# Mixture of experts in a decoder layer: large experts as 128 split rows and 64 unsplit rows, another expert order, 16 KB weight pieces, 16-bit biases

## Chip, cores and metric

The kernel runs on one core of a Trainium2 chip. The metric is the time of one execution on the device in microseconds; a kernel's time is the median of its runs.

## What is computed

One decoder layer for 512 tokens of width 1024, in fp32: a token mixer (differential attention beside a gated MLP, one input and one output projection), a layer norm, a router that picks 4 of 32 experts for each token, the experts, a second layer norm. The change concerns the experts and the few steps ahead of them. Cut to that part, the reference is:

```python
logits = xt @ w_router + b_router
topv, topi = lax.top_k(logits, TOP_K)              # 4 of 32
gates = jax.nn.softmax(topv, axis=-1)
def expert_block(args):                            # rows of one expert
    xb, e = args
    h = xb @ w_up[e] + b_up[e]                     # 1024 -> 2 x 1024
    ...                                            # clamped SwiGLU -> 1024
    return a @ w_down[e] + b_down[e]               # 1024 -> 1024
```

Each token's output is the sum of its four experts' rows times their gates. An expert's weights are 8 MB for up (gate and linear columns) and 4 MB for down, so the layer reads some 400 MB of weights.

## The kernel before

**Exactness.** A matmul of fp32 operands is made in one of two ways. *Split*: the weights and the rows are each cut into a high part rounded to fp32r (a cast by ScalarE, L149) and a low rest (a subtraction by VectorE, L150), and three fp32r matmuls (high by high, high by low, low by high) are summed in PSUM. *Unsplit*: the fp32 weights go to TensorE as they are loaded, with 64 rows as stationary columns; the two halves of the output columns go to the two column halves of the array (`tiled_mm`, L1417), and no cast or subtraction is needed.

**Slots.** The experts are sorted by their number of rows on the device. One expert is fixed and comes first, the others follow in an order of ranks that is written into the kernel (`ORDER`); a rank has a fixed capacity (`CAP_STEPS`). Up to 64 rows make an *L* slot (16 of them), unsplit. 65 to 128 rows make an *M* slot (the fixed one and 11 more), split, six matmuls of 512 columns for each chunk (L1454 up, L1493 down). Over 128 rows make an *H* slot (ranks 1 to 4, capacities 256, 192, 176, 160): two row blocks, both split, on quarters of the up columns and halves of the down columns (`wide_mm`: L1344 for a full block; for a second block of up to 64 rows L1334 and L1338, whose stationary holds high and low rows side by side, so that the sum of the low half is later folded in by L1363 after a one-column matmul L1326).

**Chunks, loads and queues.** A slot has 16 up chunks and 8 down chunks of 128 by 1024 weights. The work list runs up of slot n, then down of slot n-1 (for H mixed in quarters). A slot's weights come as four up and two down loads of 2 MB into six raw buffers, released in order; SyncE issues the next load when the oldest buffer is released: at the split of its last chunk for M and H (`emit_splits`, `used`), after the last matmul for L. Splits are made three chunks ahead (LEAD). An M load takes two whole weight rows of a partition (16 KB) per piece (`wu_l`, `wd_l`), an L load 8 KB or 4 KB (`wu_t`, `wd_t`), an H load 1 KB or 2 KB (`wu_h`, `wd_h`, L675).

**PSUM.** PG holds the gate sums, PL the linear ones, PD the down sums, each 128 by 1024; X0 and X1 take transposes and lists. M and H use all of PG, PL and PD; an L slot uses one 512-column half, alternating. At the end of down, ScalarE scales PD into a buffer (`out_a`, L1400 for L and M, L1406 for H), and GpSimd scatters it into the accumulator in DRAM.

**Biases.** `bias_rows` makes a table from the up biases: a VectorE addition over 64 rows (L885), a cast to fp32r (L887), two subtractions (L890). An M slot adds them by two fp32r matmuls over 64 rows for gate and for linear (L1317), an L slot by two fp32 matmuls each (L1423), an H slot by L1322. `bias_rows` stands in the middle of the routing stretch: on ScalarE, L887 comes ahead of the copies L794 of the transposed hidden rows, which the router's matmul L799 needs; on VectorE, L885 and L890 come ahead of the second layer-norm tile (L777).

Of the kernel before, what the change touches and what calls it, by code (L numbers as in the profile page):

```python
# [34 lines left out]
CAP_STEPS = ((0, 128), (1, 256), (2, 192), (3, 176), (4, 160), (5, 128), (6, 120), (7, 112), (8, 104), (9, 96), (11, 88), (12, 80), (15, 72),  # L35
# [21 lines left out]
ORDER = "LLMLMHLMMMLMHLLMMLLLHMLLMLHLMLL"  # L57
# [9 lines left out]
def moe_layer(ctx, tc, x, w_in, lambda_q1, lambda_k1, lambda_q2, lambda_k2, subln_g, gmlp_ln_g,  # L67
# [10 lines left out]
    xb = [X0, X1]  # L78
    count = {}
# [5 lines left out]
    def xbank():  # L85
        return xb[nxt("x", 2)]
# [572 lines left out]
    wu_l = w_up[0].rearrange("e (p k) f -> e p k f", p=128)  # L659
    wu_h = w_up[0].rearrange("e (p k) (g c f) -> e p k g c f", p=128, g=2, c=4)  # L660
    wd_l = w_down[0].rearrange("e (p k) f -> e p k f", p=128)
    wd_h = w_down[0].rearrange("e (p k) (c f) -> e p k c f", p=128, c=2)
# [4 lines left out]
    def load_up(e, part, heavy, tiled=False):  # L667
        raw = raw_tile()
        if tiled:
            dst = raw.rearrange("p (k f) -> p k f", k=2)  # L670
            nc.sync.dma_start(dst, wu_t[e, :, part * 2:part * 2 + 2].rearrange("o p k f -> (o p) k f"))
        elif heavy:
            dst = raw.rearrange("p (k g f) -> p k g f", k=8, g=2)
            for g in range(2):
                nc.sync.dma_start(dst[:, :, g], wu_h[e, :, :, g, part].rearrange("o p k f -> (o p) k f"))  # L675
        else:
            dst = raw.rearrange("p (k f) -> p k f", k=2)
            nc.sync.dma_start(dst, wu_l[e, :, part * 2:part * 2 + 2].rearrange("o p k f -> (o p) k f"))
        return raw

    def load_down(e, part, heavy, pieces=1, tiled=False):
        raw = raw_tile()
        if tiled:
            src = wd_t[e, :, part * 4:part * 4 + 4]
            dst = raw.rearrange("p (k f) -> p k f", k=4)
        elif heavy:
            src = wd_h[e, :, :, part]
            dst = raw.rearrange("p (k f) -> p k f", k=8)
        else:
            src = wd_l[e, :, part * 4:part * 4 + 4]  # L690
            dst = raw.rearrange("p (k f) -> p k f", k=4)
        src = src.rearrange("o p k f -> (o p) k f")
        m = src.shape[1] // pieces
        for j in range(pieces):
            nc.sync.dma_start(dst[:, j * m:(j + 1) * m], src[:, j * m:(j + 1) * m])
        return raw
# [3 lines left out]
    x1v = x1.rearrange("p i (q k) -> p i q k", k=8)  # L700
    xrs = [view(W, i * 1024, 1024) for i in range(2)]
# [11 lines left out]
    tb = types.SimpleNamespace()  # L713
# [123 lines left out]
    def first_rows(i, ks):  # L837

        for k in ks:
            nc.tensor.matmul(xP[:, k], x1v[:, i, :, k], tb.oh0[:, i].bitcast(F32),  # L840
                             start=(i == 0 and k % 4 == 0), stop=(i == 3 and k % 4 == 3))
# [40 lines left out]
    def bias_rows():  # L882

        braw = tb.braw
# [10 lines left out]
    def first_loads(parts):  # L895
        for kind, part in parts:
            raw_of[(0, kind, part)] = (load_up if kind == "u" else load_down)(slot_expert(0), part, False)

    def norm_loads():
# [5 lines left out]
        tb.braw = view(tb.rt, 1024, 1024)  # L905
# [4 lines left out]
        for b in range(4):  # L910
            rows = slice(b * 32, (b + 1) * 32)
            nc.sync.dma_start(tb.braw[rows], b_up[0][:, (b // 2) * 1024:(b // 2) * 1024 + 1024])
# [67 lines left out]
    def first_x():  # L980

        xh, xl = t_buf(128, False)
        slots[0].xT.append((xh, xl))
# [64 lines left out]
    heavy = [r for r in range(1, NE) if capacity(r) > 128]  # L1048
    onehot = words("p64", 32, F32R)
    onehot_h = words("p64h", 2 * len(heavy), F32R).rearrange("p (g s) -> p g s", g=2)  # L1050
    onehot_t = words("p64t", 64).rearrange("p (g s) -> p g s", g=2)
# [70 lines left out]
    def tables_d():  # L1122
        P4 = tb.P4
        nc.vector.tensor_scalar(onehot_h[:, 1], P4[:, heavy[0]:heavy[-1] + 1], bge[:, 2:3], None, op0=OP.mult)
        nc.vector.tensor_tensor(onehot_h[:, 0], P4[:, heavy[0]:heavy[-1] + 1], onehot_h[:, 1].bitcast(F32),
                                op=OP.subtract)
        nc.vector.tensor_scalar(onehot_t[:, 1], P4, bge[:, 2:3], None, op0=OP.mult)
        nc.vector.tensor_tensor(onehot_t[:, 0], P4, onehot_t[:, 1], op=OP.subtract)
        tb.zeros = words("zeros", 128, BF16)
        nc.vector.memset(tb.zeros, 0.0)  # L1130
        tb.low_ident = words("lowid", 64, F32R)
        nc.vector.tensor_copy(tb.low_ident, ident[:, 64:128])

    def first_list():
# [4 lines left out]
        slots[0].lists.append((idx, gt))  # L1139
# [11 lines left out]
    def list_mask(s, blk, rows):  # L1151
        if blk == 0:
            nc.vector.tensor_tensor(tb.oh[:, :, 0:rows], iota[:, 0:rows].unsqueeze(1).to_broadcast([128, 4, rows]),
                                    tb.posm_s[:, :, s:s + 1].to_broadcast([128, 4, rows]), op=OP.is_equal)
            return
        for i in range(NT):
            nc.vector.tensor_scalar(tb.oh[:, i, 0:rows], iota[:, 0:rows], 128.0 * blk, tb.posm_s[:, i, s:s + 1],
                                    op0=OP.add, op1=OP.is_equal)
# [7 lines left out]
    def mask_h(s):  # L1166
        nc.vector.tensor_tensor(tb.oh.rearrange("p i (c r) -> p i c r", c=2),
                                iota[:, 0:64].unsqueeze(1).unsqueeze(1).to_broadcast([128, 4, 2, 64]),
                                tb.posm_s[:, :, s:s + 1].unsqueeze(3).to_broadcast([128, 4, 2, 64]), op=OP.is_equal)
# [27 lines left out]
    def transpose_h(src, eng, dst=None, js=slice(0, 4)):  # L1197
# [3 lines left out]
        tp = xbank().rearrange("p (j r) -> p j r", j=4)  # L1201
        for j in range(js.start, js.stop):
            nc.tensor.transpose(tp[:, j], src[:, j * 128:(j + 1) * 128], ident)
# [21 lines left out]
    def transpose_half(dst, src, hf, rows, stacked):  # L1225

        sv = src.rearrange("p (q k) -> p q k", k=8)
        tp = xbank()[:, 0:4 * rows].rearrange("p (k t) -> p k t", k=4)
        for k in range(4):
            nc.tensor.transpose(tp[:, k], sv[:, :, hf * 4 + k], ident[0:rows, 0:rows])  # L1230
        ks = slice(hf * 4, hf * 4 + 4)
        if stacked:
            split_to(dst[0][:, ks, 0:rows], dst[0][:, ks, 64:64 + rows], tp)
        else:
            split_to(dst[0][:, ks], dst[1][:, ks], tp)

    def t_buf(rows, stacked):
        j = nxt("tb", 4)
        hi = view(BC, j * 1024, 8, 128)
        if stacked:  # L1240
            return hi, view(words(f"low{j}", 1024), 0, 8, 64)
        return hi[:, :, 0:rows], view(words(f"low{j}", 1024, F32R), 0, 8, 128)[:, :, 0:rows]
# [6 lines left out]
    act2b = view(W, 2048, 2, 1024)  # L1249

    class Slot:
        def __init__(self, s):
            self.s = s
            self.nblk = (capacity(s) + 127) // 128
            self.rows = [min(128, capacity(s) - 128 * b) for b in range(self.nblk)]
            self.halves = [r <= 64 for r in self.rows]
            self.last = s == slot_order()[-1]

            self.tiled = self.halves[0]
            assert self.tiled or not self.last  # L1260
            h = slice(512, 1024) if self.tiled and nxt("tiled", 2) else slice(0, 512)
            self.hg, self.hl, self.hd = PG[:, h], PL[:, h], PD[:, h]
            self.down_psum = PD
            self.lists, self.xg, self.xT, self.aT, self.y = [], [], [], [], []

        def mask(self, b):
            if self.tiled:
                mask_h(self.s)
            else:
                list_mask(self.s, b, self.rows[b])  # L1270

        def fetch(self, b):
            if self.last:
                self.lists.append(full_list(self.s))
                self.xg.append(gather_h(self.lists[0][0]))
                return
            if self.tiled:
# [714 lines left out]
```

## Time and profile before

| | |
|---|---|
| runs | 1487.75, 1485.09, 1482.64 us, median 1485.09 us |
| profiled execution | 1484.02 us, span 1481.9 us, mean granted clock 0.978 |
| TensorE busy | 1404.2 us, 95% of the span |
| VectorE, ScalarE busy | 798.3 us (54%), 612.2 us (41%) |
| queue of the weight loads | 435.75 MB, 76.0% of 16 engines' span |
| experts on TensorE | first matmul at 274.1 us, last at about 1454.4 us |

An engine's busy time is what its instructions took; TensorE's matmuls overlap, so their price is the distance from one start to the next. The span begins with the first instruction; the execution's own time is 2.1 us longer than the span. The stretch before 274 us is the token mixer, the layer norm and the routing; after 1454 us comes the last accumulation and layer norm.

### The profile page before, as it was taken

How to read it: one execution, taken by the hardware profiler on the slowest of the kernel's cores; microseconds unless marked ns; L12 is line 12 of the kernel's file. 1: busy time of each engine (PE TensorE's matmuls, PEld its weight loads, DVE VectorE, ACT ScalarE, POOL GpSimd, SP SyncE). 2: the span in 40 equal slices, each digit the busy share in tenths (PEclk: the TensorE clock that was granted, in tenths of full speed). 3: DMA queues.
4: the chain of work that ended last, by engine and by line, in shares of the span. 5: the costliest groups of instructions: out<-in, count | busy, mean ns of one | idle time of the engine just before them, and what ended most of it. 6: DMA issues, size and time to landing. Idle time of an engine off the chain costs nothing. (4 is left out here: it accounts for less than half of the span.)

```text
span 1481.9 us, 17074 instructions
## 1 busy us (share of the span) xinstructions
PE 1404.2 (95%) x6494; PEld 872.9 (59%) x6494; DVE 798.3 (54%) x1237; ACT 612.2 (41%) x813; POOL 135.8 (9%) x136
## 2 busy tenths in 40 slices
PE   8999999899998999999999999996999999999992
PEld 6877778645655867675666545542666453656430
DVE  4455668643656545786855347531554363635324
ACT  3354541322544434574644345421454252526212
POOL 0000000032010010001100010010000120000210
PEclk9999999899999999999999999999999999999996
DMA  9030154569999979999996989999986999999994
GB/s 337 12 114 1 65 178 184 212 269 399 395 417 381 367 253 323 385 381 368 377 386 232 364 321 415 413 399 381 389 293 266 362 411 394 379 349 348 380 403 150
DMA packets 109717, 461.39 MB, mean 311 GB/s; under 512 B 7808, under 2 KB 41856, under 8 KB 84032
## 3 DMA queue, kind: packets, MB, share of 16 engines
q1 hardware_dynamic: 101328, 435.75, 76.0%
q0 software_dynamic: 8304, 24.52, 6.7%
q8 instruction: 52, 0.85, 0.2%
q14 instruction: 33, 0.27, 0.0%
HBM read 440.23 MB, written 20.00 MB: 311 GB/s over the span
## 5 line engine op out<-in xcount | busy, mean ns | idle before, releaser
L150 DVE TENSOR_TENSOR ring<-raw,ring 128x1024 fp32r<-128x1024 f32 (+1 forms) x400 | 468.6, 1208 | 178.3 <-ACT ring L149 172.2
L149 ACT CAST ring<-raw 128x1024 fp32r<-128x1024 f32 (+1 forms) x400 | 400.9, 1039 | 144.3 <-DMA raw<-in_w_up_dram 24.0
L1417 PE MATMUL PG<-raw,low 128*64 128x512 f32 x512 | 135.1, 605 | 5.3 <-DMA raw<-in_w_up_dram 3.1
L1417 PE MATMUL PL<-raw,low 128*64 128x512 f32 x512 | 132.9, 597 | 0.0
L1417 PE MATMUL PD<-raw,low 128*64 128x512 f32 x512 | 124.2, 616 | 3.2 <-DMA raw<-in_w_down_dram 1.7
L1382 ACT ACTIVATE PG<-PG 128x512 f32<-128x512 f32 (+9 forms) x37 | 26.1, 706 | 203.6 <-PE PG L1417 122.5
L150 DVE TENSOR_TENSOR low<-X,bc 128x512 fp32r<-128x512 f32 (+7 forms) x66 | 39.5, 599 | 130.9 <-ACT bc L149 130.9
L1454 PE MATMUL PG<-ring,bc 128*80 128x512 f32 (+7 forms) x384 | 108.5, 404 | 1.4 <-DVE ring L150 0.9
L1493 PE MATMUL PD<-ring,bc 128*80 128x512 f32 (+7 forms) x384 | 107.2, 400 | 2.3 <-ACT ring L149 1.7
L1454 PE MATMUL PL<-ring,bc 128*80 128x512 f32 (+7 forms) x384 | 107.0, 401 | 1.7 <-DVE w L1387 1.7
L149 ACT CAST bc<-X 128x512 fp32r<-128x512 f32 (+10 forms) x78 | 37.8, 484 | 145.0 <-PE X L1230 144.4
L1454 PEld LDWEIGHTS PG<-ring,bc 128*80 128x80 f32 (+7 forms) x384 | 60.5, 165 | 32.1 <-issue 7.9
L1454 PEld LDWEIGHTS PL<-ring,bc 128*80 128x80 f32 (+7 forms) x384 | 61.2, 165 | 29.8 <-issue 4.9
L1493 PEld LDWEIGHTS PD<-ring,bc 128*80 128x80 f32 (+7 forms) x384 | 60.8, 164 | 30.6 <-ACT PG L1382 3.2
L1383 DVE TENSOR_SCALAR w<-PL 128x512 f32<-128x512 f32 (+9 forms) x36 | 30.1, 836 | 86.8 <-PE PL L1454 39.9
L1230 PEld LDWEIGHTS X<-ident,w 128*128 128x128 f32 (+10 forms) x304 | 41.5, 197 | 55.2 <-issue 26.2
L1417 PEld LDWEIGHTS PL<-raw,low 128*64 128x64 f32 x512 | 35.2, 137 | 63.0 <-issue 62.3
L1417 PEld LDWEIGHTS PD<-raw,low 128*64 128x64 f32 x512 | 33.9, 140 | 60.6 <-issue 55.4
L1417 PEld LDWEIGHTS PG<-raw,low 128*64 128x64 f32 x512 | 32.8, 136 | 61.3 <-issue 53.1
L1189 POOL DMA_INDIRECT w<-x1d,small x15 | 18.1, 1207 | 553.5 <-DMA raw<-in_w_up_dram 276.0
L1230 PE MATMUL X<-ident,w 128*128 128x128 f32 (+10 forms) x304 | 49.9, 287 | 12.4 <-DVE low L150 12.4
L1454 PE MATMUL PG<-ring,low 128*80 128x512 f32 (+7 forms) x192 | 60.4, 396 | 0.3 <-DVE low L985 0.3
(497 smaller groups left out, 2167.1 us busy)
## 6 DMA issues: line engine op xcount, KB each, us to landing
raw<-in_w_up_dram SPq DMA_DIRECT2D x112, 2048.0 KB, 13.4
raw<-in_w_down_dram SPq DMA_DIRECT2D x64, 2048.0 KB, 14.1
raw<-in_w_up_dram SPq DMA_DIRECT2D x32, 1024.0 KB, 15.9
raw<-in_w_in_dram SPq DMA_DIRECT2D x8, 1024.0 KB, 11.5
raw<-in_w_o_dram SPq DMA_DIRECT2D x2, 2048.0 KB, 9.0
raw<-in_x_dram SPq DMA_DIRECT2D x4, 512.0 KB, 6.4
raw<-in_w_in_dram SPq DMA_DIRECT2D x4, 512.0 KB, 9.2
w<-in_x_dram SPq DMA_DIRECT2D x4, 512.0 KB
```

Of the source, the lines that this page charges most:

```text
L149: nc.scalar.copy(hi, src)
L150: eng.tensor_tensor(lo, src, hi.bitcast(F32), op=OP.subtract)
L1189: nc.gpsimd.indirect_dma_start(out=xg, out_offset=None, in_=x1d_h, in_offset=bass.IndirectOffsetOnAxis(ap=idx, axis=0))
L1230: nc.tensor.transpose(tp[:, k], sv[:, :, hf * 4 + k], ident[0:rows, 0:rows])
L1382: nc.scalar.activation(pg, pg, AF.Silu, scale=SWIGLU)
L1383: nc.vector.tensor_scalar(l, pl, LIMIT + 1.0, 1.0 - LIMIT, op0=OP.min, op1=OP.max)
L1417: nc.tensor.matmul(P[64 * c:64 * c + 64], T[:, k], w[:, c * 512:(c + 1) * 512], start=(k == 0 and not started), stop=(k == 7))
L1454: nc.tensor.matmul(P[:, cs], x_[:, kt], w_[:, cs], start=(kt == 0 and n == 0), stop=(kt == 7 and n == 2))
L1493: nc.tensor.matmul(P[:, cs], a_[:, k], w_[:, cs], start=(k == 0 and n == 0), stop=(k == 7 and n == 2))
```

## The change

H slots get one capacity, 192. The first 128 rows are split as in an M slot (`full_mm`), the other 64 rows are unsplit as in an L slot (`half_mm`), and both are made for each chunk of weights: six fp32r matmuls and one pair of fp32 column-half matmuls. The 64 rows' gate and linear sums lie in the halves of PD and their down sum in X1; an L slot ahead of an H slot also puts its down sum in X1, and transposes have X0 alone meanwhile. An H load's buffer is released after its last matmul rather than at its split. The order is new, with no two H side by side and no H after an M. Every load now takes 16 KB of contiguous weights per partition (`wu_v`, `wd_v`), so the transposes of rows pick strided columns. The bias table becomes three bf16 rows (high, middle, low) of 2048 columns for each expert, added for all slots by bf16 matmuls over 96 rows (`half_bias`, `full_bias`).

```diff
-CAP_STEPS = ((0, 128), (1, 256), (2, 192), (3, 176), (4, 160), (5, 128), ...
+CAP_STEPS = ((0, 128), (1, 192), (5, 128), ...
-ORDER = "LLMLMHLMMMLMHLLMMLLLHMLLMLHLMLL"
+ORDER = "LMLHLMLMLMLHLMLMLMLHLMLMMLMLHLL"
+assert "HH" not in ORDER and "MH" not in ORDER and ORDER[-1] == "L"
...
-    wu_t = w_up[0].rearrange("e (k p) f -> e p k f", p=128)
-    wd_t = w_down[0].rearrange("e (k p) f -> e p k f", p=128)
+    wu_v = w_up[0].rearrange("e (c p j) f -> e c p j f", c=2, j=4)
+    wd_v = w_down[0].rearrange("e (c p j) f -> e c p j f", c=2, j=4)
...
     def bias_rows():
-        nc.vector.tensor_scalar_add(braw[64:128], braw[64:128], 1.0)
-        tb.bup = bup = words("bup", 1024, F32R)
-        nc.scalar.copy(bup, braw)
-        for b in (1, 3):
-            rows = slice(b * 32, (b + 1) * 32)
-            nc.vector.tensor_tensor(bup[rows], braw[rows], bup[rows].bitcast(F32), op=OP.subtract)
+        tb.bup = bup = words("bup", 2048, BF16)
+        nc.vector.tensor_scalar_add(tb.braw[1], tb.braw[1], 1.0)
+        for n in range(2):
+            b, part = tb.braw[n], bup[0:96, n * 1024:n * 1024 + 1024]
+            nc.scalar.copy(part, b)
+            for p0 in (32, 64):
+                rows = slice(p0, p0 + 32)
+                nc.vector.tensor_tensor(b[rows], b[rows], part[rows], op=OP.subtract)
+                nc.scalar.copy(part[rows], b[rows])
+            rows = slice(64, 96)
+            nc.vector.tensor_tensor(b[rows], b[rows], part[rows], op=OP.subtract)
+            nc.scalar.copy(part[rows], b[rows])
...
+            if self.wide:
+                self.hg, self.hl, self.hd = PD[:, 0:512], PD[:, 512:1024], X1
+            elif self.half:
+                h = slice(512, 1024) if nxt("tiled", 2) else slice(0, 512)
+                self.hg, self.hl, self.hd = PG[:, h], PL[:, h], PD[:, h]
+                if not self.last and capacity(order[n + 1]) > 128:
+                    self.hd = X1
...
+                    def mm(w, hi, lo, kt=kt, gl=gl):
+                        if self.full:
+                            P = (PG, PL)[gl]
+                            if kt == 7:
+                                self.full_bias(P, gl)
+                            self.full_mm(P, self.xT[0], kt, hi, lo)
+                        if self.half:
                             P = (self.hg, self.hl)[gl]
-                            self.tiled_mm(P, self.xT[0], kt, w)
+                            self.half_mm(P, self.xT[-1], kt, w)
                             if kt == 0:
-                                self.tiled_bias(P, gl)
+                                self.half_bias(P, gl)
...
-                ready[emitted[0]] = split_ring(src(raw_of[key + (part,)]), *shape)
-                used(key + (part,))
+                ready[emitted[0]] = (raw,) + split_ring(raw, *shape)
+                if not slots[key[0]].half:
+                    used(key + (part,))
```

**Where instructions move.** The first place is `bias_rows` on ScalarE, in the routing stretch. Before, one cast of the bias table stands ahead of the copies of the hidden rows:

```order
134 L153 CAST bc_71<-X_65 128x4x128
135 L887 CAST bup_1644<-ring_48_1528 128x1024
136 L794 COPY ring_46_1526<-X_64 128x512
137 L794 COPY ring_46_1526<-X_65 128x512
138 L800 COPY r_109<-X_64 128x32
```

With the change, eight stand there (L774 is the copy that was L794):

```order
135 L869 CAST bup_1643<-ring_46_1526 96x1024
136 L873 CAST bup_1643<-ring_46_1526 32x1024 x2
137 L876 CAST bup_1643<-ring_46_1526 32x1024
138 L869 CAST bup_1643<-ring_44_1524 96x1024
139 L873 CAST bup_1643<-ring_44_1524 32x1024 x2
140 L876 CAST bup_1643<-ring_44_1524 32x1024
141 L774 COPY ring_44_1524<-X_64 128x512
142 L774 COPY ring_44_1524<-X_65 128x512
```

On VectorE in the same place, the change has one addition (L866) and six subtractions ahead of the next layer-norm tile (L757, which was L777), where before it were one addition and two subtractions:

```order
282 L866 TENSOR_SCALAR ring_44_1524<-ring_44_1524 96x1024
283 L872 TENSOR_TENSOR ring_46_1526<-ring_46_1526,bup_1643 32x1024 x2
284 L875 TENSOR_TENSOR ring_46_1526<-ring_46_1526,bup_1643 32x1024
285 L872 TENSOR_TENSOR ring_44_1524<-ring_44_1524,bup_1643 32x1024 x2
286 L875 TENSOR_TENSOR ring_44_1524<-ring_44_1524,bup_1643 32x1024
287 L757 SCALAR_TENSOR_TENSOR w_76<-w_76,PG 128x1024
```

So each of these queues carries a chain in which cast and subtraction take turns, ahead of work that the router waits for. The other place is an H slot on TensorE. Before, two row blocks share a chunk (the last rows of an up quarter and the fold of the one before it):

```order
1720 L1363 MATMUL PG<-ring_60_1980,lowid_2071 64x512
1721 L1344 MATMUL PL<-ring_53_1831,bc_71 128x512 x2
1722 L1344 MATMUL PL<-ring_53_1831,low_169_4775 128x512
1723 L1334 MATMUL PL<-ring_53_1831,bc_71 128x512
1724 L1338 MATMUL PL<-ring_53_1831,bc_71 64x512
```

With the change, the end of the down chunks of the slot before (PD) and the first up chunks of the H slot:

```order
1111 L1347 MATMUL PD<-ring_60_2053,bc_71 128x512 x4
1112 L1347 MATMUL PD<-ring_60_2053,low_87_2656 128x512 x2
1113 L1347 MATMUL PG<-ring_54_1969,bc_71 128x512 x4
1114 L1347 MATMUL PG<-ring_54_1969,low_92_2736 128x512 x2
1115 L1333 MATMUL PD<-raw_86_2654,low_94_2783 64x512 x2
1116 L1340 LDWEIGHTS p_36_674
1117 L1340 MATMUL PD<-bup_1643,p_36_674 64x512
1118 L1340 LDWEIGHTS p_36_674
1119 L1340 MATMUL PD<-bup_1643,p_36_674 64x512
1120 L1347 MATMUL PL<-ring_58_1991,bc_71 128x512 x4
1121 L1347 MATMUL PL<-ring_58_1991,low_92_2736 128x512 x2
1122 L1333 MATMUL PD<-raw_86_2654,low_94_2783 64x512 x2
```

Fp32r matmuls (L1347) and fp32 column-half matmuls (L1333) now alternate in every chunk of an H slot, and the first L1333 writes the PD that the down chunks just ahead have filled.

## Rows read from the trace of the kernel before

**Rows 1.** Busy time in the expert stretch: stretch, length, busy time (instructions) by engine, clock, DMA.
```profile
274.10:1454.40 1180.30, 1147.23 (x5180) 662.16 (x5180) 621.29 (x801) 502.81 (x596) 130.22 (x116) 0.99 0.96 360
```

**Rows 2.** Waits of TensorE between 280 and 1450 us: total us, times, longest us.
```profile
PE X L1230 <- DVE low L150: 12.4, 3, 7.9
...
PE PG L1417 <- DMA raw<-in_w_up_dram: 3.1, 3, 1.5
...
PE PD L1417 <- DMA raw<-in_w_down_dram: 1.7, 2, 1.0
...
PE PD L1417 <- ACT k L1400: 1.2, 1, 1.2
```

**Rows 3.** Routing stretch on VectorE: start, duration, engine, line, operation, count.
```profile
222.88 0.69 DVE L885 TENSOR_SCALAR ring<-ring 64x1024 f32<-64x1024 f32 x1
224.69 2.47 DVE L890 TENSOR_TENSOR bup<-ring,bup 32x1024 fp32r<-32x1024 f32 x2 [1.12 <-ACT bup L887]
227.18 1.22 DVE L777 SCALAR_TENSOR_TENSOR w<-w,PG 128x1024 f32<-128x1024 f32 x1
```

**Rows 4.** The same stretch on ScalarE.
```profile
223.60 1.05 ACT L887 CAST bup<-ring 128x1024 fp32r<-128x1024 f32 x1 [4.36 <-DVE ring L885]
224.56 1.06 ACT L794 COPY ring<-X 128x512 f32<-128x512 f32 x2
```

**Rows 5.** The same stretch on TensorE.
```profile
226.35 1.87 PE L799 MATMUL X<-r,ring 128*128 128x32 f32 x16
...
249.16 0.43 PE L824 MATMUL X<-k,oh 128*128 128x96 f32 x2 [1.52 <-DVE k L817]
```

**Rows 6.** TensorE after a long wait, timeline of 472 to 478 us.
```profile
476.51 1.12 PE L1230 MATMUL X<-ident,w 128*128 128x128 f32 x4 [3.74 <-DVE low L150]
```

**Rows 7.** Busy time after that wait (columns as in the first group).
```profile
478.00:482.00 4.00, 4.00 (x12) 0.95 (x8) 1.92 (x3) 0.25 (x1) 0.00 (x0) 0.56 1.02 429
```

**Rows 8.** TensorE in an L slot, timeline from 1426 us.
```profile
1427.71 1.03 PE L1423 MATMUL PG<-bup,p64t 128*64 128x512 f32 x4
1428.57 1.03 PE L1417 MATMUL PL<-raw,low 128*64 128x512 f32 x4
```

**Rows 9.** TensorE in an M slot's last up chunks, timeline from 303 us.
```profile
303.58 0.73 PE L1317 MATMUL PG<-bup,p 64*128 64x512 f32 x2
...
305.83 0.73 PE L1317 MATMUL PL<-bup,p 64*128 64x512 f32 x2
```

**Rows 10.** TensorE in an H slot, timeline from 1308 us.
```profile
1308.93 0.44 PE L1363 MATMUL PG<-ring,lowid 32*64 32x512 f32 x1
1309.30 0.73 PE L1344 MATMUL PL<-ring,bc 128*128 128x512 f32 x2
1309.87 0.40 PE L1344 MATMUL PL<-ring,low 128*128 128x512 f32 x1
1310.10 0.39 PE L1334 MATMUL PL<-ring,bc 128*128 128x512 f32 x1
```

**Rows 11.** TensorE where L work meets M work, timeline from 1405 us.
```profile
1405.61 1.03 PE L1417 MATMUL PL<-raw,low 128*64 128x512 f32 x4
1406.57 1.15 PE L1493 MATMUL PD<-ring,bc 128*72 128x512 f32 x4
...
1408.02 1.08 PE L1493 MATMUL PD<-ring,bc 128*72 128x512 f32 x4
```

**Rows 12.** TensorE where M work meets L work, timeline from 465 us.
```profile
465.33 0.62 PE L1454 MATMUL PL<-ring,low 128*120 128x512 f32 x2
465.88 1.94 PE L1417 MATMUL PD<-raw,low 128*64 128x512 f32 x8
```

**Rows 13.** Weight queue from 963 to 1029 us, L slots: packets, MB, share of 16 engines.
```profile
q1 hardware_dynamic: 4900, 24.20, 91.6%
```

**Rows 14.** Weight queue from 596 to 640 us, M slots.
```profile
q1 hardware_dynamic: 1104, 16.17, 89.7%
```

**Rows 15.** Weight queue from 1043 to 1063 us, an H slot.
```profile
q1 hardware_dynamic: 4744, 7.06, 99.8%
```

More of the change, by code (lines that the diff above doesn't have):

```diff
@@ L1045, in routing @@
         nc.sync.dma_start(bd, b_down[0])
[L1048 to L1051, printed above, removed]
+    onehot = words("p64", 32, BF16)
     def counts():
@@ L1248, in moe_layer, with __init__ @@
     act2 = [view(W, 2048, 1024), view(W, 3072, 1024)]
-    act2b = view(W, 2048, 2, 1024)
     class Slot:
-        def __init__(self, s):
+        def __init__(self, n, s):
+            order = slot_order()
             self.s = s
[L1254 to L1264, printed above, removed]
+            cap = capacity(s)
+            self.full = 0 if cap <= 64 else min(128, cap)
+            self.half = cap <= 64 or cap > 128
+            self.wide = cap > 128
+            assert cap <= 192
+            self.last = n == len(order) - 1
+            assert not (self.last and self.full)
+            self.parts = [0, 128] if self.wide else [0]
+            if self.wide:
[5 more added lines that the diff above has]
+                    self.hd = X1
+            self.nparts = len(self.parts)
+            self.lists, self.xg, self.xT, self.aT, self.y = ([None] * self.nparts for _ in range(5))
@@ L1266, in mask, with is_half @@
+        def is_half(self, b):
+            return self.half and b == self.nparts - 1
         def mask(self, b):
-            if self.tiled:
-                mask_h(self.s)
+            if self.is_half(b):
+                mask_h(self.s, self.parts[b])
             else:
-                list_mask(self.s, b, self.rows[b])
+                list_mask(self.s, self.full)
         def fetch(self, b):
             if self.last:
-                self.lists.append(full_list(self.s))
-                self.xg.append(gather_h(self.lists[0][0]))
-                return
@@ new lines, in full_mm, with full_bias @@
+        def full_mm(self, P, T, k, hi, lo):
+            xh, xl = T
+            for n, (x_, w_) in enumerate(((xh, hi), (xh, lo), (xl, hi))):
+                for c in range(2):
+                    cs = slice(c * 512, (c + 1) * 512)
+                    nc.tensor.matmul(P[0:self.full, cs], x_[:, k], w_[:, cs], start=(k == 0 and n == 0),
+                                     stop=(k == 7 and n == 2))
+        def full_bias(self, P, gl):
+            lhs = onehot[0:96, self.s:self.s + 1].to_broadcast([96, self.full])
+            for c in range(2):
+                c0 = gl * 1024 + c * 512
+                nc.tensor.matmul(P[0:self.full, c * 512:c * 512 + 512], lhs, tb.bup[0:96, c0:c0 + 512], start=False,
+                                 stop=False)
@@ new lines, in down_chunks, with mm, src @@
+            for k in range(KT):
+                def mm(w, hi, lo, k=k):
+                    if self.hd_taken():
+                        tb.x1_taken = True
+                    if self.full:
+                        self.full_mm(PD, self.aT[0], k, hi, lo)
+                    if self.half:
+                        self.half_mm(self.hd, self.aT[-1], k, w, self.last)
+                def src(t, k=k):
+                    return t[:, (k % 4) * 1024:(k % 4) * 1024 + 1024]
+                out_.append((k // 4, src, (1024,) if self.full else None, mm))
@@ L1512, in down_chunks @@
             return out_
-    slots = [Slot(r) for r in slot_order()]
+    slots = [Slot(n, s) for n, s in enumerate(slot_order())]
     N = len(slots)
@@ L1636, in at @@
         events.setdefault(c, []).append((lead, f))
-    def place_folds(every=False):
-        while folds and (every or len(stream) >= folds[0][0] + folds[0][3]):
-            after, key, (copies, mm), _ = folds.pop(0)
-            where[key] = len(stream)
-            stream.append((None, (after, copies, None, mm)))
     def add(n, kind, part):
@@ L1653, in add @@
             stream.append(((n, kind), c))
[L1654 to L1662 removed]
+        if part == ch[-1][0]:
+            where[(n, kind, "sum")] = len(stream) - 1
     chunks = {}
@@ L1707, in moe_layer @@
+        c = where[(n, "d", "sum")]
+        at(c, lambda sl=sl: sl.out_a(), LEAD)
+        at(c + 1, lambda sl=sl: sl.out_b(), L)
     ready = {}
@@ L1711, in moe_layer @@
     for key, (part, *_) in stream:
[L1712 to L1713 removed]
+        uses[key + (part,)] = uses.get(key + (part,), 0) + 1
     def used(load):
@@ L1877, in moe_layer @@
             mm(*ready.pop(c))
-            if key is not None and shape is None:
+            if slots[key[0]].half:
                 used(key + (part,))
```

429 lines of the change are left out of this document (119 added, 310 removed).

## The prediction

> **What bounds the kernel now.** The busy times of the engines come first: TensorE is busy for most of the span. The same view of the expert stretch alone says where it isn't: 1147.2 of 1180.3 us, with the DMA engines at 0.96 too [rows 1]. So TensorE sets the pace, and the weight loads are so close behind that each microsecond taken from TensorE must be checked against them. The table of TensorE's waits then says what stops it: it names VectorE's low part for 12.4 us and loads directly for 3.1 and 1.7 us [rows 2]. Followed back, the 12.4 us are late weights as well, since the transposes stand behind splits that wait for a buffer: 17.2 us in all. Behind such a wait TensorE is slow: after 3.74 us of idleness [rows 6] the granted clock of the next 4 us is 0.56 of the upper level of 2.4 GHz, so mostly the lower one, 1.2 [rows 7]; 4 x 0.44 makes some 2 us. There were two such waits, 4 us. Last, the timelines give prices as distances between starts.
>
> **Unit prices.** An fp32r matmul of 512 columns takes 0.23 us [rows 10]. A pair of unsplit matmuls for an L chunk takes 0.86 us, and so does an L bias [rows 8]. Two M biases with the six matmuls between them take 2.25 us [rows 9]; less 6 x 0.23 = 1.38 this leaves 0.87 for a bias and what it does to its neighbours. Where L work meets M work the last L chunk takes 0.96 instead of 0.86 and the first M chunk 1.45 instead of 1.38 [rows 11]. The other way, the last two M matmuls take 0.55 instead of 0.46, and the next two L chunks last 1.94 us instead of 1.03 + 0.86 [rows 12, 8]. The round trip costs 0.10 + 0.07 + 0.09 + 0.05 = 0.31 us, one way 0.155.
>
> **The change, term by term.**
>
> *1. The bias table: +12 us.* Only the routing stretch pays it. VectorE's addition ends at 223.57 [rows 3]. After it the two queues take turns: a subtraction lasts 2.47 / 2 = 1.23 us [rows 3], a cast 1.05 [rows 4]. Subtract, subtract (226.1), cast (227.2), subtract (228.4), cast (229.5), the second half's first cast (230.6), subtract, subtract (233.1), cast (234.2), subtract (235.4), cast (236.5). Then the copies of hidden rows, 1.06 us [rows 4], end at 237.6. The router's matmul, which began at 226.35 [rows 5], is in order on TensorE, so all projections behind it wait 11.3 us; VectorE's next tile moves from 227.18 [rows 3] to 235.4 only. Some 2 us at the lower clock follow [rows 7]. TensorE had 1.52 us to spare where it next met VectorE [rows 5], which covers that much: 11.3 + 2 - 1.5 = 12. Ends: 0, if the matmuls make it up before the tail of the routing, which VectorE sets; +16, if the narrower casts cost more.
>
> *2. L biases in bf16: -19 us.* There are 16 x 2 of them. An fp32 bias costs 0.86 [rows 8]. No row shows a bf16 matmul of this width; the nearest is fp32r's 0.23 [rows 10], and the two column halves may run side by side as the fp32 pair does. I take 0.25: 32 x 0.61 = 19. Ends: -21 (0.20) and 0, should it take the fp32 time.
>
> *3. M biases over 96 rows: -10 us.* 12 x 2 of them, from 0.87 [rows 9] to two matmuls of 0.23 without the step to a 64-row stationary: 24 x 0.41 = 10. Ends 0 (the step is paid for 96 rows too) and -13.
>
> *4. H arithmetic: -28 us.* Before: three experts of 48 steps x 5 matmuls and one of 48 x 6, 1008 x 0.23 = 232; 64 half-width biases at half of that, 7; 18 folds at 0.37 [rows 10], 7; 18 one-column matmuls, taken at 0.1, 2. Sum 248. After: 4 x 24 chunks x (1.38 + 0.86) = 215, and 4 x 2 x (0.46 + 0.25) = 6 for biases. Sum 221, so about -28. A further 32 transposes of 128 columns go, a quarter of 0.23 each: -2.
>
> *5. Type changes: +26 us.* Counted along the program, work passes between unsplit and split chunks 49 times before and 215 times after, of which 188 are inside H slots: 166 x 0.155 = 26. Ends: +14 if weights of the next chunk are loaded under the last one, +55 if each costs twice as much, as the fp32 stationaries here belong to other row sets. The Trainium skill's page TensorEngine Tiling (Array Packing), section Key Properties, says that a change of tiling mode drains TensorE, which speaks against exactly this mixing; by it nothing of the 26 could be hidden. The trace agrees in that each passage costs something [rows 11, 12].
>
> *6. PD's eviction: +2 us.* The first L1333 of an H slot writes the PD which the M slot before it just filled. In the same situation TensorE once waited 1.2 us for ScalarE's eviction [rows 2]. Here 1.38 us of L1347 lie between, which cover most; half a microsecond for each of four slots. Ends 0 and +8 (two casts of 1.05 ahead of the eviction). Behind that wait stands all of the H slot.
>
> *7. Weights in time: -4 us.* The queue moved 24.20 MB in 66 us at 91.6% [rows 13], 16.17 MB in 44 at 89.7% [rows 14], 7.06 MB in 20 at 99.8% [rows 15]: 400, 410 and 354 GB/s at full share. With 16 KB pieces all should do 410 and leave a tenth to gathers and scatters: 12.58 MB in 34 us. An L slot then has 25 us on TensorE, an M slot 36, an H slot 62. Three pairs of L and M and one L between two H slots lack 3 x 7 + 9 = 30 us, and an H slot refills 28, with what the six buffers hold beyond it. That is just about even: I leave 4 us of waiting in each of four stretches, 16, against 17.2 + 4 before. Ends -21 and +10. The Trainium skill's page DMA: Bandwidth & Descriptors, section Specifications, puts line rate at 512 bytes and up; by that alone larger pieces bring nothing, this term would be 0 and the sum -19. Here the 1 KB pieces ran at 354 GB/s and the 16 KB ones at 410, so the trace differs.
>
> Sum: 12 - 19 - 10 - 28 - 2 + 26 + 2 - 4 = -23, against the profiled execution's 1484.0 us (span 1481.9 and 2.1 us around it): 1461. That execution lies 1.1 us under the median of the runs, so the forecast is **1462 us**.
>
> **Rivals.**
> - *Prefetch runs out: 1478 us.* An H part now holds its buffer until its last matmul, some three chunks of 2.5 us later than at its split. If the 7.5 us of lead that this costs is missing at the end of two of the four stretches, 16 us come on top: 1478. For it speaks the DMA's 0.96; against it that H slots bring 28 us of slack each.
> - *H slots pay for mixing: 1492 us, slower.* In each of 96 H chunks the step to unsplit columns and back costs 0.63 us instead of 0.31: +30. It decides from +0.29 us a chunk, where the gain of 23 and the bound of measurement are used up. For it: the rows price only changes between long runs of one type. Against it: rows 11 and 12 have the same stationaries and moving types.
> - *The routing delay is hidden and waits vanish: 1442 us.* The 12 us shrink to 5 and the waiting to 3: -20. For it: the spare time at the next meeting with VectorE; against it: the whole chain is serial.
> - *The change does not do what it says*: bf16 biases that run at the fp32 price give back 19 us, 1481.
>
> **How the numbers follow.** Forecast (1452 to 1472): 0.55. Prefetch runs out: 0.15. Mixing: 0.13. Routing hidden: 0.12. Biases at the old price: 0.05. The range 1441 to 1488 takes in all but the slow case and the outer parts of the others. About 0.3%, or 4.4 us, is what a measurement here tells from no change: faster means under 1480.7. The forecast and the hidden case count as faster, with two thirds of the prefetch case and half of the last: 0.79. Within the bound: the rest of these and a little of the mixing case, 0.10. Slower: 0.11.
>
> **What would show it.** Right: the router's matmul at about 237.6, behind casts, and a lower clock after it; an L bias at a quarter of an L chunk; an H chunk of 2.5 us, evenly; TensorE's waits in the expert stretch at 15 to 20 us, at the end of stretches of L and M. Wrong: an H chunk over 2.85 us, waits for loads over 35 us, a routing stretch that is no later, or an L bias still at 0.86 us.

## The result, and the profile after

The changed kernel takes 1448.51 us (median of 4 runs, 1446.65 to 1449.89) against 1485.17 before in the same session: ratio 0.9753, 95% interval [0.9735, 0.9772]. The forecast was 1462 in a range of 1441 to 1488. The direction was right and the time lies in the range, but 37 us went where 23 were forecast.

The profiled execution has a span of 1448.2 us, 33.7 less than before. Three marks divide the difference: the first expert matmul, the last up chunk of the last expert, and the end. The stretch between the first two (columns as in rows 1), before:

```profile
274.10:1441.95 1167.85, 1137.45 (x5136) 659.16 (x5138) 617.43 (x790) 496.14 (x583) 130.22 (x116) 0.99 0.96 360
```

and after:

```profile
290.55:1400.76 1110.21, 1098.02 (x4925) 588.95 (x4927) 608.69 (x756) 479.11 (x537) 111.38 (x108) 1.00 0.95 379
```

The experts lost 57.6 us (1167.85 less 1110.21), of which 39.4 are TensorE's busy time and 18.2 its idleness. Ahead of them 16.4 us were added, behind them 7.5 (39.95 us from the second mark to the end before, 47.44 after): -57.6 + 16.4 + 7.5 = -33.7.

TensorE's waits from 280 to 1450 us, the answer to [rows 2]:

```profile
PE PD L1678 <- DMA w<-accd,r: 13.6, 1, 13.6
PE X L1687 <- DVE small L1685: 6.7, 1, 6.7
PE PD L1347 <- ACT ring L152: 3.3, 2, 1.7
PE X L1075 <- DVE r L835: 3.2, 1, 3.2
...
PE PG L1333 <- DMA raw<-in_w_up_dram: 1.1, 2, 0.6
PE X L1179 <- DVE low L1180: 0.8, 1, 0.8
```

Under the names that made 17.2 us before, late weights are 1.9 us now (1.1 and 0.8). The two waits on a cast, 3.3 us, are late weights too, since those casts (L152 at 687.89 and 964.10) had themselves stood idle for 10.34 and 10.11 us for a down load; with 1.1 us on the subtractions behind them this makes 6.3 us. Counted the same way, before has 2.3 more (1.69 and 0.57 on L1493), 19.5. Behind the last up chunk TensorE waits for the readback of the accumulator and then for a last step of VectorE, 13.6 and 6.7 us. Before, the readback cost 2.3 us and the last step more:

```profile
PE PD L1832 <- DMA w<-accd,r: 2.3, 1, 2.3
```

```profile
1466.49 0.59 PE L1841 MATMUL X<-small,oh 128*128 128x2 f32 x2 [12.14 <-DVE small L1839]
```

So the two waits together grew by 5.9 us, from 14.4 to 20.3.

The routing stretch on ScalarE, the answer to [rows 4]:

```profile
222.60 0.59 ACT L156 CAST bc<-X 128x512 fp32r<-128x512 f32 x1 [2.20 <-PE X L548]
223.09 1.04 ACT L869 CAST bup<-ring 96x1024 bf16<-96x1024 f32 x1
228.66 1.04 ACT L873 CAST bup<-ring 32x1024 bf16<-32x1024 f32 x1 [4.53 <-DVE ring L872]
...
239.19 1.04 ACT L876 CAST bup<-ring 32x1024 bf16<-32x1024 f32 x1 [1.28 <-DVE ring L875]
240.26 1.07 ACT L774 COPY ring<-X 128x512 f32<-128x512 f32 x2
```

and on TensorE, the answer to [rows 5]:

```profile
240.90 3.62 PE L779 MATMUL X<-r,ring 128*128 128x32 f32 x16 [10.44 <-ACT ring L774]
...
266.04 0.43 PE L804 MATMUL X<-k,oh 128*128 128x96 f32 x2 [0.27 <-DVE k L797]
```

Casts and subtractions take turns as forecast; the router's matmul waits 10.44 us and then runs for 3.62 instead of 1.87 us. The granted clock from 240.9 to 244.9 us is 0.50 (the lower level, 1.2 GHz); before, from 226.3 to 230.3 us, it was 1.00.

The unit prices on TensorE. An L slot's first chunks, the answer to [rows 8], with the bias pair L1340 0.22 us long from start to start (1388.01 less 1387.79):

```profile
1386.93 1.03 PE L1333 MATMUL PG<-raw,low 128*64 128x512 f32 x4
1387.79 0.39 PE L1340 MATMUL PG<-bup,p 96*64 96x512 bf16 x2
1388.01 1.03 PE L1333 MATMUL PL<-raw,low 128*64 128x512 f32 x4
```

An M slot's biases (L1354), the answer to [rows 9]; from bias to bias 1.82 us, less 1.38 for six matmuls, 0.44 each instead of 0.87:

```profile
318.92 0.61 PE L1354 MATMUL PG<-bup,p 96*128 96x512 bf16 x2
319.18 1.26 PE L1347 MATMUL PG<-ring,bc 128*128 128x512 f32 x4
...
320.74 0.61 PE L1354 MATMUL PL<-bup,p 96*128 96x512 bf16 x2
```

An H slot's up chunks; from one L1333 to the next 2.59 us:

```profile
441.05 1.08 PE L1333 MATMUL PD<-raw,low 128*64 128x512 f32 x4
442.06 1.19 PE L1347 MATMUL PG<-ring,bc 128*128 128x512 f32 x4
443.09 0.62 PE L1347 MATMUL PG<-ring,low 128*128 128x512 f32 x2
443.64 1.08 PE L1333 MATMUL PD<-raw,low 128*64 128x512 f32 x4
```

### The profile page after: what moved, and what is told of

Read it like the earlier page. It is cut to its first block, busy times and chain, and to the rows that moved or that the text cites. A ratio compares the mean times of both kernels' runs of the same rounds, so it can differ in the third digit from the quotient of the medians.

```text
span 1448.2 us, 16516 instructions
## 1 busy us (share of the span) xinstructions
PE 1374.1 (95%) x6282; PEld 808.7 (56%) x6282; DVE 794.4 (55%) x1207; ACT 602.5 (42%) x774; POOL 119.5 (8%) x130
## 5 line engine op out<-in xcount | busy, mean ns | idle before, releaser
L152 ACT CAST ring<-raw 128x1024 fp32r<-128x1024 f32 (+1 forms) x400 | 399.7, 1039 | 182.3 <-PE PG L1347 51.5
L1333 PE MATMUL PD<-raw,low 128*64 128x512 f32 x640 | 157.7, 608 | 0.3 <-ACT w L1320 0.2
L1347 PE MATMUL PD<-ring,bc 128*128 128x512 f32 (+7 forms) x512 | 147.1, 407 | 4.6 <-ACT ring L152 3.3
L1347 PE MATMUL PG<-ring,bc 128*128 128x512 f32 (+7 forms) x512 | 147.3, 409 | 0.6 <-ACT bc L971 0.5
L1347 PE MATMUL PL<-ring,bc 128*128 128x512 f32 (+7 forms) x512 | 146.7, 408 | 0.0
L1333 PE MATMUL PG<-raw,low 128*64 128x512 f32 x512 | 133.6, 600 | 3.0 <-issue 2.0
L1333 PE MATMUL PL<-raw,low 128*64 128x512 f32 x512 | 132.5, 596 | 0.0
L1347 PEld LDWEIGHTS PD<-ring,bc 128*128 128x128 f32 (+7 forms) x512 | 81.8, 172 | 59.5 <-ACT ring L152 13.2
L1347 PEld LDWEIGHTS PG<-ring,bc 128*128 128x128 f32 (+7 forms) x512 | 84.5, 171 | 47.5 <-issue 18.7
L1347 PEld LDWEIGHTS PL<-ring,bc 128*128 128x128 f32 (+7 forms) x512 | 84.2, 171 | 47.0 <-issue 18.7
L152 ACT CAST bc<-X 128x512 fp32r<-128x512 f32 (+7 forms) x62 | 31.7, 511 | 139.5 <-PE X L1206 139.5
L1347 PE MATMUL PG<-ring,low 128*128 128x512 f32 (+7 forms) x256 | 80.3, 395 | 0.3 <-DVE low L972 0.3
L1347 PE MATMUL PD<-ring,low 128*128 128x512 f32 (+7 forms) x256 | 80.0, 393 | 0.0
L1347 PE MATMUL PL<-ring,low 128*128 128x512 f32 (+7 forms) x256 | 80.0, 393 | 0.0
L1333 PEld LDWEIGHTS PD<-raw,low 128*64 128x64 f32 x640 | 37.9, 136 | 69.4 <-issue 65.1
L1333 PEld LDWEIGHTS PL<-raw,low 128*64 128x64 f32 x512 | 35.2, 136 | 61.0 <-issue 59.5
L1333 PEld LDWEIGHTS PG<-raw,low 128*64 128x64 f32 x512 | 33.4, 136 | 58.2 <-issue 50.7
```

The lines of the kernel that those rows point to most:

```text
L152: nc.scalar.copy(hi, src)
L1333: nc.tensor.matmul(P[64 * c:64 * c + 64], T[:, k], w[:, c * 512:(c + 1) * 512], start=(k == 0 and not started), stop=(k == 7))
L1347: nc.tensor.matmul(P[0:self.full, cs], x_[:, k], w_[:, cs], start=(k == 0 and n == 0), stop=(k == 7 and n == 2))
```

## The experiments

All ratios are to the kernel before on the same chip. Differences to the changed kernel compare medians of different sessions, in which the kernel before had medians of 1483.35 to 1486.77 us; so a gain of 4 us is hardly more than what sessions differ by, and there the profile's stretches decide. Three questions: what took the waits for weights away, what the routing stretch and the end cost, and what mixing costs in an H slot.

**Order alone, in the kernel before.** Only its `ORDER` becomes the evenly spread one of the run on the end, below.

```diff
-ORDER = "LLMLMHLMMMLMHLLMMLLLHMLLMLHLMLL"
+ORDER = "LMLHLMLMLMLHLMLMLMLHLMLMLHLMMLL"
```

> The kernel before with an evenly spread order (that of the run in which the last H slot comes earlier), nothing else changed. Theory B: TensorE's waits named for VectorE's low part and for weights, 17 us in the expert stretch before, fall under 8, and the time by 10 to 18 us. Theory A: with pieces of 1 to 8 KB the waits stay over 12 us, and the time is within 6 us of before.

Measured: 1455.44 us, ratio 0.9809 [0.9774, 0.9844], 28 us faster by this line alone. Its expert stretch:

```profile
274.42:1411.51 1137.09, 1126.29 (x5137) 656.65 (x5139) 616.52 (x790) 497.40 (x583) 139.64 (x116) 1.00 0.98 371
```

30.8 us less than before: idleness falls from 30.4 to 10.8 us, and busy time by 11.2. By an estimate from the granted clocks some 4 us of that are the slow matmuls behind the two waits ([rows 7]; 0.55 from 1037.72 to 1041.72, where this run has 1.00), and some 3 us a lower clock near the start (0.86 from 282 to 300 us and 0.91 from 300 to 320, against 0.94 and 1.00). The rest was not traced. No wait named for the loads themselves is left, and of the 12.4 us that TensorE waited for VectorE's low part only this:

```profile
PE X L1230 <- DVE low L150: 1.0, 2, 0.8
```

Theory B holds, with more than its upper end; the pieces are not needed for it in this kernel.

**The clustered order in the changed kernel.**

```diff
-ORDER = "LMLHLMLMLMLHLMLMLMLHLMLMMLMLHLL"
+ORDER = "LLMMLHLMMMMLHLLMMLLLHMLLMLHLMLL"
```

> The changed kernel with nearly the order of before: the L and M slots clustered as there, M and L exchanged ahead of an H slot where the new kernel needs an L there. Theory B (the even spread of H slots took the waits for weights away): TensorE's waits for weights between the first expert matmul and the last up chunk come back to 10 us or more, and this stretch, 1110.2 us in the changed kernel's profile, takes 10 to 20 us more; the end gains some 4 us, as no H slot is among the last three. Theory A (the pieces did it): this stretch is within 4 us.

Measured: 1457.58 us, 0.9824 [0.9791, 0.9856], 9 us slower than the changed kernel. Stretch and waits:

```profile
289.99:1410.58 1120.59, 1102.16 (x4924) 589.78 (x4926) 608.25 (x756) 476.53 (x537) 120.31 (x109) 0.99 0.94 375
```

```profile
PE PG L1333 <- DMA raw<-in_w_up_dram: 6.2, 4, 2.3
...
PE PD L1333 <- DMA raw<-in_w_down_dram: 2.0, 2, 1.4
PE PG L1347 <- ACT ring L152: 1.9, 1, 1.9
```

The stretch takes 10.4 us more, at the lower end of theory B; direct waits for weights come to 8.2 us, just under the 10 expected. The end is 3.3 us shorter (44.1 instead of 47.4), near the 4 expected.

**Small pieces in the changed kernel.** The up loads of H slots go in pieces of 1 KB and those of L slots in pieces of 8 KB; the down loads, not shown in the cut, go likewise in 2 KB and 4 KB.

```diff
+        if capacity(s) > 128:
+            dst, src = (t.rearrange("p k f -> p (k f)").rearrange("p (r h f) -> p h r f", r=8, h=2) for t in (dst, src))
+            for n in range(2):
+                nc.sync.dma_start(dst[:, n], src[:, n])
+        elif capacity(s) <= 64:
+            for n in range(2):
+                nc.sync.dma_start(dst[:, n], src[:, n])
...
```

> The changed kernel with small pieces again: H loads as two transfers of 1 KB (up) and 2 KB (down) pieces, L loads as two of 8 KB and 4 KB pieces; the same bytes to the same places. Theory A (the waits for weights went because larger pieces move faster): H loads run at some 354 GB/s again, TensorE's waits for weights in the expert stretch come back to 10 us or more, and the time rises by 8 to 20 us. Theory B (they went because the H slots, which need fewer bytes per microsecond, are now spread evenly): the time rises by under 4 us.

Measured: 1459.29 us, 0.9823 [0.98, 0.9845], 11 us slower than the changed kernel. While an H slot's weights come in, the queue moves this from 399 to 421 us (packets, MB, share of 16 engines):

```profile
q1 hardware_dynamic: 5312, 7.27, 95.5%
```

and this from 402 to 424 in the changed kernel:

```profile
q1 hardware_dynamic: 589, 8.57, 91.8%
```

At full share that is 7.27 / (22 x 0.955) = 346 GB/s against 8.57 / (22 x 0.918) = 424. The stretch:

```profile
286.75:1408.64 1121.89, 1103.76 (x4924) 592.75 (x4926) 608.06 (x756) 479.94 (x537) 112.68 (x108) 0.99 0.98 375
```

11.7 us more, and 18.1 us idle instead of 12.2. TensorE's waits for weights are back as well, behind casts that waited for down loads (L1366 is L1347):

```profile
PE PD L1366 <- ACT ring L152: 9.5, 4, 3.0
```

So theory A holds in the changed kernel too: neither order nor pieces alone is the cause there. Why small pieces cost this much here, while the kernel before in a spread order kept them with 10.8 us of idleness, was not tried.

**Both.** The two edits above together.

> The changed kernel with both the clustered order and the small pieces. Alone they cost some 10 us each in the expert stretch. If they draw on the same lead of the loads, the sum is more than additive: the stretch takes 25 to 40 us more than the 1110.2 of the changed kernel, with 20 us or more of TensorE's waits for weights. If they are independent, 20 to 23 us more. The end gains 2 to 4 us as in the run with the order alone.

Measured: 1466.96 us, 0.9868 [0.9836, 0.9901].

```profile
287.31:1418.75 1131.44, 1104.10 (x4925) 589.64 (x4927) 608.00 (x756) 476.23 (x537) 123.30 (x110) 0.99 0.97 370
```

21.2 us more than the changed kernel, the sum of 10.4 and 11.7 within a microsecond: in the changed kernel the two are independent. Idleness is 27.3 us, near the 30.4 of before. The end, 46.1 us, gains 1.4 and not the 2 to 4 expected. Counted this way, the rest of the change is worth 1167.85 - 1131.44 = 36.4 us in this stretch. Counted from the other side, order alone took 30.8 us off the kernel before, and all the rest of the change, pieces included, took only 26.3 more in that same order (1137.09 to the 1110.80 of the run on the end). What order is worth, 30.8 or 10.4 us, thus depends on what else has been changed.

**The bias table early.** `bias_rows()` is called after `mix_gated(1)`, ahead of the output projection's last blocks.

> The bias table is built from the same instructions, but ahead of the last blocks of the output projection instead of in the routing stretch; all else is the changed kernel. In the changed kernel the experts start at 290.55 us, 16.45 later than before. Theory (the chain of casts and subtractions, in order on ScalarE and VectorE, holds the copies of hidden rows and so the router's matmul): the wait of 10.44 us before that matmul goes, the first expert matmul is at 274 to 278, the time falls by 11 to 16 us. Rival (TensorE or VectorE would be late there anyway, from the longer list of small steps): it falls by under 4 us.

Measured: 1444.55 us, 0.9731 [0.9704, 0.9758], 4 us faster than the changed kernel: a miss, between theory and rival. The first expert matmul is at 282.82, not at 274 to 278. The chain now stood ahead of another step that TensorE needs; on VectorE, L543 began at 223.11, when the chain's last subtraction (221.86, 1.22 us long) had ended:

```profile
223.86 0.48 PE L548 MATMUL X<-ident,ring 128*128 128x128 f32 x1 [8.97 <-DVE ring L543]
```

**The bias table on GpSimd.** In `bias_rows`, `nc.vector` and `nc.scalar.copy` become `nc.gpsimd` and `nc.gpsimd.tensor_copy`.

> The bias table's additions, casts and subtractions all on GpSimd, in the same place of the program; GpSimd is busy for 8% of the span. Theory (the delay is the chain in ScalarE's and VectorE's queues ahead of the router): the copies of hidden rows start at about 224 again, the first expert matmul is at 273 to 278, and the time falls by 10 to 15 us, as long as GpSimd ends before the first bias matmul, some 45 us after the experts start. Moved earlier as a whole, the chain had only stood ahead of another step, the gated MLP's. Rival (GpSimd is so slow, or disturbs VectorE so much, that the table is late): no gain, and a wait at the first bias matmul.

Measured: 1444.07 us, 0.9729 [0.9698, 0.976], again only 4 us. VectorE's four weight subtractions in that stretch took

```profile
204.35 9.93 DVE L153 TENSOR_TENSOR raw<-raw,raw 128x1024 fp32r<-128x1024 f32 x4 [0.20 <-ACT raw L152]
```

while GpSimd worked, and in the changed kernel

```profile
207.79 4.63 DVE L153 TENSOR_TENSOR raw<-raw,raw 128x1024 fp32r<-128x1024 f32 x4 [0.19 <-ACT raw L152]
```

In this stretch GpSimd slows VectorE to half, and TensorE waits for VectorE there instead of at the router:

```profile
215.78 1.12 PE L548 MATMUL X<-ident,ring 128*128 128x128 f32 x4 [7.43 <-DVE ring L543]
```

The first expert matmul is at 282.74, not at 273 to 278. So the theory misses by what the rival said of VectorE, but the table was not late: no bias matmul is among TensorE's waits. The Trainium skill's page GPSIMD Engine Reference, section Specifications, says that GpSimd shares its SBUF interface with VectorE and names instructions with two SBUF inputs; these have two, and the trace agrees.

**The bias table in a wide layout.** The biases are loaded, and the three parts made, as 128 partitions by 512 columns; the parts are then moved into the table by 12 small transfers.

```diff
+        b, parts = tb.braw, tb.bparts
+        nc.vector.tensor_scalar_add(b[64:128], b[64:128], 1.0)
+        for n, part in enumerate(parts):
+            if n:
+                nc.vector.tensor_tensor(b, b, parts[n - 1], op=OP.subtract)
+            nc.scalar.copy(part, b)
...
+        for n, part in enumerate(tb.bparts):
+            for c in range(4):
+                nc.sync.dma_start(tb.bup[n * 32:n * 32 + 32, c * 512:c * 512 + 512], part[c * 32:c * 32 + 32])
...
```

> The bias table's three parts are made in a layout of 128 partitions by 512 columns (four column blocks of 32 experts): one addition, three casts, two subtractions, in the same place of the routing stretch, and then 12 small transfers put them into the table. The chain of the two queues shrinks from 13 to about 4 us (three casts at 0.6, two subtractions at 0.7, the addition 0.4). Theory (the router waits for that chain): TensorE's wait of 10.4 us before the router's matmul falls under 3, the experts start by 274 to 279 and the time falls by 9 to 14 us. GpSimd had slowed VectorE down in the run that moved the chain there, so this is the first run that shortens it. Rival (something else in this stretch has become late): under 5 us.

Measured: 1437.22 us, 0.9659 [0.9626, 0.9692], 11.3 us faster than the changed kernel. ScalarE and TensorE there:

```profile
226.65 0.62 ACT L870 CAST ring<-ring 128x512 bf16<-128x512 f32 x1 [4.09 <-DVE ring L866]
...
229.40 0.62 ACT L870 CAST ring<-ring 128x512 bf16<-128x512 f32 x1 [0.76 <-DVE ring L869]
```

```profile
230.56 1.97 PE L779 MATMUL X<-r,ring 128*128 128x32 f32 x16 [0.73 <-ACT ring L774]
```

The wait falls from 10.44 to 0.73 us, and the first expert matmul is at 278.38 instead of 290.55. The chain in front of the router was the cost, and its length counted more than its place.

**The end.** The last H slot comes three places earlier.

```diff
-ORDER = "LMLHLMLMLMLHLMLMLMLHLMLMMLMLHLL"
+ORDER = "LMLHLMLMLMLHLMLMLMLHLMLMLHLMMLL"
```

> Only the order's end: the last large expert comes three places earlier in the order (two places ahead of the last two M slots), so that its two scatters are not among the last ones. Theory (the 13.58 us wait for the accumulator's last rows is the queue of scatters: an H slot's two and an L slot's one, each of which waits for the one before): the wait falls to 2 to 5 us and the time by 6 to 10. Rival (the last readback is slow whatever ran before): the wait stays above 10 us and the time within 2 us.

Measured: 1444.57 us, 0.9724 [0.9701, 0.9746], 4 us faster than the changed kernel. In the changed kernel, GpSimd's queue of scatters was

```profile
1380.24 1.56 POOL L1216 DMA_INDIRECT accd<-w,small  x1 [37.31 <-ACT w L1320]
1394.12 1.55 POOL L1169 DMA_INDIRECT accd<-k,small  x1 [12.32 <-DMA accd<-w,small]
1402.94 1.55 POOL L1169 DMA_INDIRECT accd<-w,small  x1 [7.26 <-issue]
1408.45 1.02 POOL L1613 DMA_INDIRECT w<-accd,r  x1 [3.96 <-issue]
```

and in this run the readback (L1613) is issued at

```profile
1400.84 1.01 POOL L1613 DMA_INDIRECT w<-accd,r  x1 [9.67 <-DMA accd<-w,small]
```

TensorE's waits behind the last up chunk are now:

```profile
PE PD L1678 <- DMA w<-accd,r: 9.4, 1, 9.4
PE X L1687 <- DVE small L1685: 6.2, 1, 6.2
```

The wait for the readback falls from 13.6 to 9.4 us, not to 5, and the end from 47.4 to 43.1: the H slot's scatters made 4.3 of the 7.5 us by which it had grown. The stretch ahead of it is that of the changed kernel:

```profile
287.17:1397.97 1110.80, 1098.46 (x4924) 588.52 (x4926) 608.88 (x756) 478.92 (x537) 110.56 (x109) 1.00 0.95 379
```

The readback starts 11.2 us after the last scatter (1389.59 in the same view), against 5.5 in the changed kernel and 8.7 in the kernel before with the same order (1400.05 and 1408.78). Why the wait stays above the 2.3 us of the kernel before was not tried.

**Pairs in an H slot.**

```diff
-                        if self.half:
+                        if self.wide and gl == 0:
+                            self.w0 = w
+                        elif self.half:
+                            for g, wg in ((0, self.w0), (1, w)) if self.wide else ((gl, w),):
...
```

> In an H slot's up chunks the unsplit matmuls for gate and linear are made together after the split matmuls of both, so there are 8 passages to unsplit and back for each slot instead of 16; the arithmetic is the same. The price of a round trip in an H chunk is 2.59 less 1.38 and 0.86, so 0.35 us. Theory (each passage costs TensorE this much): 32 fewer round trips, -11 us in TensorE's busy time and -8 to -11 in the time. Rival (the surplus is that of reading weights from two places, or of the fp32 pair itself, and stays): within 3 us.

Measured: 1439.66 us, 0.9688 [0.9664, 0.9713], 8.9 us faster than the changed kernel. The stretch:

```profile
290.41:1389.41 1099.00, 1086.71 (x4925) 592.52 (x4926) 607.80 (x756) 478.89 (x537) 112.58 (x108) 1.00 0.96 383
```

Busy time falls by 11.3 us for 32 round trips, 0.35 each, as the theory had it.

**Together.** The table on GpSimd, pairs and the earlier H slot:

> Three edits together: the bias table on GpSimd, the unsplit matmuls of an H slot in pairs, the last H slot three places earlier. If they are independent the gains add up: some 12 + 9 + 4 = 25 us below the changed kernel, 1422 to 1428. If weights run out, because TensorE needs them faster, 8 to 15 us of it come back as waits for weights.

Measured: 1432.01 us, 0.9646 [0.9613, 0.9679]. The single gains measured were 4.4, 8.9 and 3.9, 17 in sum, and 16.5 came; the expectation had still counted 12 for the table. With the wide table instead:

> The wide bias table, the unsplit matmuls of an H slot in pairs and the last H slot three places earlier. With gains that add up: 12 + 9 + 4 below the changed kernel, 1421 to 1427 us; weights must not run out for it, as they did not with the table on GpSimd (1432).

Measured: **1423.78 us**, 0.9567 [0.9532, 0.9602], 25 us below the changed kernel and 63 below the one before: the fastest version here. Gains add up (11.3 + 8.9 + 3.9 = 24), and weights don't run out: direct waits for them are 0.9 us.

## Why the prediction was right or wrong

- **Term 1, routing, +12: right.** The changed kernel's first expert matmul is 16.4 us later, but 3.9 of that is there before the chain begins: the cast ahead of it ends its wait at 222.60, and at 218.66 before. Runs with the same instructions there show both values (218.39 in the run on the end, 222.51 in the run on pairs). 12.5 us remain, and shortening the chain gave 11.3 back.
- **Terms 2 and 3, biases, -19 and -10: right.** 32 x (0.86 - 0.22) = 20.5 and 24 x (0.87 - 0.44) = 10.3.
- **Terms 4 and 5, H slots, -28 - 2 + 26 = -4: a little too good.** Term 4's own figures add up to -27. The kernel before in the spread order and the run on the end have the same order; their busy times are 1126.3 and 1098.5 us (1098.46 of 1110.80 in the latter). Of those 27.8 us the biases are 30.8, so the rest of the H change, folds and transposes included, costs 3 rather than saving 4. By an estimate from the granted clocks some 2 of the 7 between them are not the kernel's (0.89 from 314 to 330 us in the run on the end, 1.00 from 300 to 400 in the other). A chunk takes 2.59 instead of 2.55 us, which over 96 chunks is another 4. The round trip measured 0.35, not 0.31. The rival at 0.63 fell.
- **Term 6, PD's eviction, +2:** between L1347 at 426.60 and the first L1333 of an H slot there is no wait; its whole cost in the waits of that line is 0.2 us.
- **Term 7, weights, -4: the step that failed.** The prediction left 16 us of waits, as "just about even"; 6.3 came. The run with both edits undone says -21.2 for the whole term, the lower end of the bounds. Two things were mis-sized. The first is what larger pieces give: 11.7 us in the changed kernel. In the one window shown the queue did 424 GB/s where 410 was taken, so 12.58 MB take 12.58 / 0.424 / 0.918 = 32.3 us and not 34; over the eight slots from one H to the next that would be 14 us more lead, against 4 us that were left as waiting there. From 600 to 640 us the same division gives only 407 (15.07 MB at 92.5%), so how much of it was the rate is not shown. The second is the clustered order itself: in the kernel before, the order alone removed 19.6 us of idleness at the old pieces. The prediction worked out the balance of the new order and never that of the old one, which would have shown what the clusters cost.
- **The end, not costed: +7.5.** The prediction named no term behind the last up chunk. An H slot's two scatters among the last three made 4.3 of it; where the other 3.2 come from stays open.

The sum as it came: -57.6 for the experts, +12.5 for the table, +7.5 for the end, and +3.9 that came before all of it. Of the 57.6, 21.2 went with order and pieces; the other 36.4 are arithmetic and biases for 27.8, by the pair of runs in the same order, and 8.6 that no run assigns. For the experts the prediction's terms 2 to 7 add up to -35, so they were 23 us too small; that the sum in the profile is only 11 us off (33.7 against 23) is in part luck, since the 11.4 us of the end and of the early clock, which no term had, went the other way. The rivals *prefetch runs out*, *mixing* and *routing hidden* did not occur, nor did biases at the old price.

## What to carry to other kernels

Where loads nearly keep up with the bound engine, look at the order of the work first: in the kernel before, spreading the slots that need few bytes per microsecond was worth 28 us at no cost, nearly as much as all the bias arithmetic gave; in the changed kernel, where larger pieces helped too, clustering them again cost 9. A preparation that is off the bound engine still costs nearly its whole length if it stands ahead of that engine's next input in an in-order queue. Here, making it short (all 128 partitions, fewer columns) gave 11 us; moving it earlier or to GpSimd gave 4 each. And after a gain in the middle, look at the end: the last scatters and readback are a chain of their own.

## What was not expected of the hardware

The same instructions ran at different granted clocks. From 120 to 160 us nothing differs in the program between the changed kernel and the run on the end. Yet in the changed kernel's profile TensorE did 182 matmuls at a clock of 0.83 (columns as in rows 1):

```profile
120.00:160.00 40.00, 38.34 (x182) 29.59 (x181) 20.95 (x52) 15.11 (x40) 0.00 (x0) 0.83 0.00 1
```

and in the profile of the run on the end 204 at 0.91:

```profile
120.00:160.00 40.00, 38.34 (x204) 30.04 (x204) 22.76 (x60) 17.47 (x45) 0.00 (x0) 0.91 0.00 1
```

At 0.19 us for each (38.34 / 204) the 22 matmuls are, by estimate, the 3.9 us: a single profile's early stretch can differ by as much as a small experiment's effect.

A cast of 32 partitions by 1024 columns took as long as one of 96, 1.04 us, and by 512 columns one of 128 partitions took 0.62. A subtraction of 32 partitions by 1024 columns took 1.23 us [rows 3], one of 128 partitions 1.16 (4.63 for four).
